# A grouped softmax on one core: four tiles instead of six, loops that cover all rows, and no inner block barrier

## Chip, cores and metric

One core of one Trainium2 chip. The metric is the device time in microseconds (us).

## The reference

The input is 4 x 4096 x 4352 float32. Each row of 4352 is split into 8 groups of 544, and a softmax is taken over each group.

```python
x_g = x.reshape(B, N, 8, 544)
x_g = x_g - x_g.max(axis=-1, keepdims=True)
exp = np.exp(x_g)
out = exp / exp.sum(axis=-1, keepdims=True)
```

Every element is read once and written once. The arithmetic is a maximum, an exponential with a sum, and a scaling.

## The kernel before

The 16384 rows are cut into 64 tiles. A tile has 128 partitions with two rows of 4352 each (4352 KB). "Row" below means one row on all 128 partitions, so there are 128 rows of work. The sync engine's queue issues all loads and stores. The vector engine takes the maximum and scales, and the scalar engine exponentiates. All arithmetic is in place in the tile.

```python
R = 2; NT = 6; S = R * NT
turns = (nr - 1) // S                    # nr = 128 rows: 10 turns of 12 rows, 8 rows left
...
ctx.enter_context(nc.cleanup_on_exit())  # clears the semaphores, then a barrier
...
with nc.Block(no_gpsimd_drain=True) as block:
    def load(t):                         # sync engine
        b = t % NT
        if t >= NT:
            sync.wait_ge(stored[b], 16 * (t // NT))
        sync.dma_start(out=bufs[b][:, :], in_=xt[t]).then_inc(landed[b], 16)
    for t in range(NT - 1):
        load(t)
    for t in range(nt):                  # nt = 64 tiles
        sync.wait_ge(scaled, R * (t + 1))
        sync.dma_start(out=ot[t], in_=bufs[t % NT][:, :]).then_inc(stored[t % NT], 16)
        if t + NT - 1 < nt:
            load(t + NT - 1)
    ...
    vector_max(0)                        # vector engine
    with loop(vector):                   # the loop's head is placed (head_slot)
        for s in range(S):
            vector_max((s + 1) % S)      # runs one row ahead, also across the loop's end
            vector_scale(s)
    for n in range(turns * S, nr): ...   # the unrolled rest; the scalar engine alike
```

`vector_scale(s)` waits for the exponentials of row s, takes 8 reciprocals in one instruction, and multiplies each group. In program order the queue issues store t, then load t + NT - 1. That load waits until store t - 1 has landed, because it goes into the same buffer.

## Time and profile before

| | before |
|---|---|
| time, median of the first 3 runs | 1330.53 us (1330.25 to 1331.39) |
| span of the profiled run | 1328.7 us |
| bytes moved | 570.43 MB in 128 transfers |
| DMA engines busy | 99.6% |
| vector / scalar engine busy | 78% / 58% |

The prediction shows the lines of the profile that carry this table. They are read in this order: which resource is always busy (the DMA engines), what the queue that feeds them waits for, and then the order of events at the start, in the middle and at the end.

### The profile page before, as it was taken

What the parts mean: (1) busy time and instruction counts of PE and PEld (TensorE: products, weight loads), DVE (VectorE), ACT (ScalarE), POOL (GpSimd) and SP (SyncE); (2) the same over time, 40 slices, a digit from 0 to 9 for tenths busy, and PEclk for the clock granted to TensorE, in tenths of its full rate; (3) what the DMA queues carried; (4) which work ended last, traced back from release to release, by engine and by line L of the source; (5) the groups of instructions that cost most, each with busy time, mean ns of one, the idle gap of its engine ahead of it and who ended that gap; (6) DMA issues with size and microseconds to landing.
All of it is one profiled execution on the core that took longest, in us unless ns stands there. A gap on an engine that the chain in (4) does not pass through costs nothing. (4 is left out here: it accounts for less than half of the span.)

```text
span 1328.7 us, 4036 instructions
## 1 busy us (share of the span) xinstructions
DVE 1041.5 (78%) x1280; ACT 764.4 (58%) x2049; POOL 0.2 (0%) x4
## 2 busy tenths in 40 slices
DVE  5999987787877878778778787787877877878770
ACT  3777765655656556555565565655655556556560
POOL 0000000000000000000000000000000000000000
DMA  9999999999999999999999999999999999999997
GB/s 401 418 434 434 434 430 428 432 436 433 435 433 431 429 436 434 436 435 430 429 436 434 435 435 432 428 435 435 434 436 434 429 431 436 434 435 434 431 430 336
DMA packets 18441, 570.51 MB, mean 429 GB/s; under 512 B 2048, under 2 KB 2048, under 8 KB 2048
## 3 DMA queue, kind: packets, MB, share of 16 engines
q1 hardware_dynamic: 18432, 570.43, 99.6%
q14 instruction: 9, 0.07, 0.0%
HBM read 285.21 MB, written 285.21 MB: 429 GB/s over the span
## 5 line engine op out<-in xcount | busy, mean ns | idle before, releaser
L72 ACT ACTIVATE xt<-xt,mx 128x544 f32<-128x544 f32 x1024 | 751.3, 735 | 528.7 <-ACTq L69 528.7
L56 DVE TENSOR_REDUCE mx<-xt 128x8 f32<-128x4352 f32 x128 | 599.1, 4680 | 234.0 <-DVEq L55 233.1
L64 DVE TENSOR_SCALAR xt<-xt,rs 128x544 f32<-128x544 f32 x1024 | 434.0, 497 | 19.2 <-DVEq L61 0.9
L72 ACT ACTIVATION_READ_ACCUMULATOR xt<-xt,mx 128x1 f32 x1024 | 191.1, 187 | 0.0
L60 DVE RECIPROCAL rs<-sm 128x8 f32<-128x8 f32 x128 | 24.5, 191 | 3.2 <-DVEq L59 3.2
L123 ACT ACT_TABLE_LOAD x1 | 1.3, 1283 | 0.9 <-SPq L36 0.9
L143 POOL MEMSET const-bfloat16-1.0<- 128x1 bf16 x1 | 0.1, 102 | 0.0
L143 POOL MEMSET const-uint8-127<- 128x1 uint8 x1 | 0.1, 102 | 0.0
L143 POOL MEMSET const-float32-0.0<- 128x1 f32 x1 | 0.1, 99 | 0.2 <-issue 0.2
L143 POOL MEMSET const-float32-1.0<- 128x1 f32 x1 | 0.1, 99 | 0.0
## 6 DMA issues: line engine op xcount, KB each, us to landing
xt<-in_x_dram SPq DMA_DIRECT2D x64, 4352.0 KB, 30.8
out_dram<-xt SPq DMA_DIRECT2D x64, 4352.0 KB, 40.7
```

The source lines that it names most:

```text
L56: nc.vector.reduce_max(out=mx[:, s, :], in_=row(s), axis=X, negate=True).then_inc(max_done, 1)
L60: nc.vector.reciprocal(out=rs[:, s, :], in_=sm[:, s, :]).then_inc(rec_done, 1)
L64: i = nc.vector.tensor_scalar_mul(out=xr[:, g, :], in0=xr[:, g, :], scalar1=rs[:, s, g:g + 1])
L72: i = nc.scalar.activation(out=xr[:, g, :], in_=xr[:, g, :], func=Exp, bias=mx[:, s, g:g + 1], scale=1.0, accum_out=sm[:, s, g:g + 1],)
L123: scalar.preload_act_table(Exp)
L143: nc = _bacc.Bacc("TRN2", target_bir_lowering=False, num_devices=1)
```

## The change

The change makes the program simpler: loops without an unrolled rest, a smaller SBUF footprint, one barrier fewer, and semaphores cleared once.

```diff
-    NT = 6
+    NT = 4
-    turns = (nr - 1) // S
+    turns = nt // NT                     # 16 turns of 8 rows, nothing left over
-    ctx.enter_context(nc.cleanup_on_exit())
-    landed = [nc.alloc_semaphore(...) ...]
+    landed = [tc.alloc_semaphore(...) ...]   # likewise the others; cleared by the context
-    with nc.Block(no_gpsimd_drain=True) as block:   # queue, vector and scalar parts inside
+    # the same queue program, issued directly
     ...
-            vector_max(0)
-            with loop(vector):
-                for s in range(S):
-                    vector_max((s + 1) % S)
-                    vector_scale(s)
-            for n in range(turns * S, nr): ...
+    with nc.vector.Fori(0, turns):           # the head's place left free
+        for s in range(S + 1):
+            if s < S:
+                vector_max(s)
+            if s:
+                vector_scale(s - 1)          # nothing runs ahead across the loop's end
```

More of the change, by code (lines that the diff above doesn't have):

```diff
@@ L6 @@
 from concourse._compat import with_exitstack
-from concourse.ordered_engine_set import OrderedEngineSet
 @with_exitstack
@@ L27 @@
     nt = N // (P * R)
-    nr = nt * R
-    turns = (nr - 1) // S
+    turns = nt // NT
+    assert turns * NT == nt
     f32 = mybir.dt.float32
@@ L34 @@
     ot = of.rearrange("(t p r) d -> t p (r d)", p=P, r=R)
+    landed = [tc.alloc_semaphore(f"landed{b}") for b in range(NT)]
+    stored = [tc.alloc_semaphore(f"stored{b}") for b in range(NT)]
+    max_done = tc.alloc_semaphore("max_done")
+    exp_done = tc.alloc_semaphore("exp_done")
+    rec_done = tc.alloc_semaphore("rec_done")
+    scaled = tc.alloc_semaphore("scaled")
     ctx.enter_context(tc.tile_critical(no_gpsimd_drain=True))
-    ctx.enter_context(nc.cleanup_on_exit())
     bufs = [ctx.enter_context(nc.sbuf_tensor(f"xt{b}", [P, R * D], f32)) for b in range(NT)]
@@ L41 @@
     rs = ctx.enter_context(nc.sbuf_tensor("rs", [P, S, G], f32))
-    landed = [nc.alloc_semaphore(f"landed{b}") for b in range(NT)]
-    stored = [nc.alloc_semaphore(f"stored{b}") for b in range(NT)]
-    max_done = nc.alloc_semaphore("max_done")
-    exp_done = nc.alloc_semaphore("exp_done")
-    rec_done = nc.alloc_semaphore("rec_done")
-    scaled = nc.alloc_semaphore("scaled")
     def row(s):
@@ L80, in scalar_exp @@
         i.then_inc(exp_done, 1)
-    def loop(engine):
-        return nc.Fori(
-            0, turns, engines=OrderedEngineSet([engine.engine]), head_slot={engine.engine: 0})
-    with nc.Block(no_gpsimd_drain=True) as block:
-        @block.sync
-        def _(sync):
-            def load(t):
-                b = t % NT
-                if t >= NT:
-                    sync.wait_ge(stored[b], 16 * (t // NT))
-                sync.dma_start(out=bufs[b][:, :], in_=xt[t]).then_inc(landed[b], 16)
-            for t in range(NT - 1):
-                load(t)
-            for t in range(nt):
-                sync.wait_ge(scaled, R * (t + 1))
-                sync.dma_start(out=ot[t], in_=bufs[t % NT][:, :]).then_inc(stored[t % NT], 16)
-                if t + NT - 1 < nt:
-                    load(t + NT - 1)
-            for b in range(NT):
-                sync.wait_ge(stored[b], 16 * ((nt - b + NT - 1) // NT))
-        @block.vector
-        def _(vector):
-            vector_max(0)
-            with loop(vector):
-                for s in range(S):
-                    vector_max((s + 1) % S)
-                    vector_scale(s)
-            for n in range(turns * S, nr):
-                if n + 1 < nr:
-                    vector_max((n + 1) % S)
-                vector_scale(n % S)
-        @block.scalar
-        def _(scalar):
-            scalar.preload_act_table(Exp)
-            with loop(scalar):
-                for s in range(S):
-                    scalar_exp(s)
-            for n in range(turns * S, nr):
-                scalar_exp(n % S)
@@ new lines, in load, with store @@
+    def load(t):
+        b = t % NT
+        if t >= NT:
+            nc.sync.wait_ge(stored[b], 16 * (t // NT))
+        nc.sync.dma_start(out=bufs[b][:, :], in_=xt[t]).then_inc(landed[b], 16)
+    def store(t):
+        nc.sync.wait_ge(scaled, R * (t + 1))
+        nc.sync.dma_start(out=ot[t], in_=bufs[t % NT][:, :]).then_inc(stored[t % NT], 16)
+    for t in range(NT - 1):
+        load(t)
+    for t in range(nt):
+        store(t)
+        if t + NT - 1 < nt:
+            load(t + NT - 1)
@@ L132 @@
+    for b in range(NT):
+        nc.sync.wait_ge(stored[b], 16 * turns)
+    nc.scalar.preload_act_table(Exp)
+    with nc.scalar.Fori(0, turns):
+        for s in range(S):
+            scalar_exp(s)
+    with nc.vector.Fori(0, turns):
[4 more added lines that the diff above has]
+                vector_scale(s - 1)
 _INS = ['x']
```

## The prediction

> **What bounds the kernel now.** I read the page first, then what the DMA queue waits for, then the vector engine and the queue in order of time. The busy rows decide little: the vector engine is busy 78%, the scalar engine 58%, and the DMA engines nearly always.
>
> ```profile
> span 1328.7 us, 4036 instructions
> ...
> DVE 1041.5 (78%) x1280; ACT 764.4 (58%) x2049; POOL 0.2 (0%) x4
> ...
> DMA  9999999999999999999999999999999999999997
> ...
> q1 hardware_dynamic: 18432, 570.43, 99.6%
> ...
> xt<-in_x_dram SPq DMA_DIRECT2D x64, 4352.0 KB, 30.8
> out_dram<-xt SPq DMA_DIRECT2D x64, 4352.0 KB, 40.7
> ```
>
> The DMA digit is 9 in every slice but the last, and the packets fill 99.6% of the 16 engines' span. So the bound is 128 transfers of 4352 KB each. What the queue waits for says the same: it waits for stores to land, hardly ever for arithmetic.
>
> ```profile
> SPq L96 <- DMA out_dram<-xt: 1141.2, 58, 20.7
> SPq L102 <- DVE xt L64: 102.4, 6, 33.3
> ```
>
> 58 of 59 later loads wait for a store to free their buffer. A store waits for arithmetic only six times, at the start and at the end. In order of time the queue and the vector engine read:
>
> ```profile
> 0.95 3.24 SPq L96 DMA_DIRECT2D xt<-in_x_dram  x5
> 37.53 0.35 SPq L102 DMA_DIRECT2D out_dram<-xt  x1
> 37.92 0.43 SPq L96 DMA_DIRECT2D xt<-in_x_dram  x1
> ...
> 596.25 4.69 DVE L56 TENSOR_REDUCE mx<-xt 128x8 f32<-128x4352 f32 x1 [3.98 <-DVEq L55]
> ...
> 616.82 4.68 DVE L56 TENSOR_REDUCE mx<-xt 128x8 f32<-128x4352 f32 x1 [3.99 <-DVEq L55]
> 621.43 0.19 DVE L60 RECIPROCAL rs<-sm 128x8 f32<-128x8 f32 x1
> 621.77 3.39 DVE L64 TENSOR_SCALAR xt<-xt,rs 128x544 f32<-128x544 f32 x8
> ...
> 1274.97 4.68 DVE L56 TENSOR_REDUCE mx<-xt 128x8 f32<-128x4352 f32 x1 [3.99 <-DVEq L55]
> ...
> 1294.49 3.39 DVE L64 TENSOR_SCALAR xt<-xt,rs 128x544 f32<-128x544 f32 x8
> ```
>
> To see: five loads go out at once, and the first store only at 37.53 us, when tile 0 is scaled. In the steady stretch one tile passes each 616.82 - 596.25 = 20.57 us, 10.28 us per transfer, and the vector engine idles 3.98 us of it. The last tile lands at about 1274.9 and is scaled by 1294.49 + 3.39 = 1297.9 us.
>
> **What the Trainium skill says.** "DMA: Bandwidth & Descriptors", Specifications, gives a fabric ceiling of 435 GB/s for the 16 engines. The trace agrees: 2 x 4352 KB (8.91 MB) in 20.57 us is 433 GB/s, so the steady stretch cannot get faster. The same page, Queues, rings and completion order, says that each engine consumes its descriptors in ring order. The trace agrees: a load lands 30.8 us after issue, which is 3 x 10.28, and a store 40.7, about 4 x 10.28, as in a first-in first-out line with two or three transfers ahead. "Runtime: NRT & Kernel Launch", Instruction fetch mechanics, warns that a taken branch out of the two-page window forces a fetch. The page here counts 9 instruction packets in all, though both loops turn 10 times, so no refetch per turn is seen before; the changed loops can test it.
>
> **The change, part by part.** Bytes, transfers, arithmetic and the alternation of loads and stores stay. I follow four parts.
>
> 1. *Four tiles, steady stretch.* Store t must be in the line before the DMA engines have emptied it. With four tiles the line after load t is store t-2, load t+1, store t-1, load t+2, store t: four transfers, 41.1 us, lie between the end of load t and the start of store t. The arithmetic of a tile, from its landing to its last scaling, takes 625.16 - 596.25 = 28.9 us, since the second row's scaling comes after the next tile's maximum. A landing comes up to some 4.2 us after most of the engines have finished that load (trace records: one engine lags), and a first packet about 1.0 us after the issue. Margin: 41.1 - 4.2 - 28.9 - 1.0 = 7.0 us. The load's side has more: load t+3 is released when store t-1 lands and still has two transfers (20.6 us) ahead. So four tiles still keep the line full. Six tiles held more than was needed: 30.8 + 28.9 + 40.7 = 100.4 us fits in five periods (102.8), and the sixth tile lay ready behind the queue's wait. Cost: 0.
>
> 2. *The loop's seam, every 8 rows.* The maximum of a turn's first row no longer runs ahead of the last scalings. For the last tile of a turn, from its landing: maximum 4.7, the previous tile's scaling to 8.3, maximum to 13.0, scaling to 16.5, then the wait for the exponentials (8 x 0.73 us after 13.1, to 19.2), scaling to 22.9 us. It is ready 6 us earlier than the others. The next tile, landed at 20.57, starts at about 23.1, 2.5 us late; its first row is scaled by 37.8 us, still before the landing after it at 41.1. So the delay is gone within that tile. 16 seams cost 0, and even a fetch of 3 us per turn would be hidden.
>
> 3. *The start.* Only three loads go out ahead of the first store. By the packet records the fourth transfer begins at 33.5 us, which is where most engines will have emptied the line. The first store goes out at 37.5 us as before (maximum, exponential and scaling of rows 0 and 1 are the same chain and need only tiles 0 and 1), first packet at 38.5. Idle: 38.5 - 33.5 = 5.0 us. After that it stays full: store 1 is ready at 54.0 and needed at 59, store 2 at 70.5 against 79.8, store 3 at 85 against 100. Cost: +5.0 us. Before, load 4 and load 5 filled this hole.
>
> 4. *The end.* Before, stores 59 to 63 lay behind the last load, and the line stayed full to the end: last landing 51.4 us after the last load's landing T (1274.83 to 1326.24 in the landing records). Now only stores 61, 62 and 63 lie behind it. Store 62 is ready at T + 8.3, in time for the lagging engine (free at T + 9.9). Store 63 is issued at T + 23.1 into an empty line (store 62 ends by T + 20.2); a lone transfer takes 13.5 us from issue to landing, as the first load did (0.95 to 14.45). So the end is T + 36.6, where a full line would give -0.4 + 3 x 10.28 + 0.3 = T + 30.8. Cost: +5.8 us.
>
> 5. *Barriers and clearing.* After the last landing the old program needs 1328.7 - 1326.2 = 2.5 us for three barriers and the clearing of semaphores. One or two barriers of some 0.4 us go, and one at the start perhaps. Gain: -0.7 us, an estimate.
>
> Check: T moves by two transfers (two of the five stores now come before the last load) and the hole: 1274.8 + 20.6 + 5.0 = 1300.4; + 36.6 = 1337.0; + 2.5 - 0.7 = 1338.8 span. The timed median lies 1.8 us over the span (1330.53 against 1328.7): **1340.5 us**, a ratio of 1.0075.
>
> **The rivals.** (a) *Four tiles are too few; the steady stretch leaves the DMA bound.* For it: the margin of 7 us is a third of a period, and five of six tiles were in use. Against: the cycle of one buffer is 30.8 + 28.9 + 13.5 (a lone store) = 73.2 us, under 4 x 20.57 = 82.3. Were I wrong by a few us of latency beyond the margin, each would cost up to 64 times: 1 us per tile is +64 us, 5% slower.
> (b) *The seam costs each turn*, by refetching the loop, whose head is no longer aligned, or by a drain. For it: the loops on both engines now have free placement. Against: the 2.5 and 3.3 us of slack computed above, and the store's own margin. If it were exposed, 16 x 2 us = +32 us, 2.4%.
> (c) *No change or faster.* If the engines started tile 0 sooner, or if the hole at the start merely let the lagging engine catch up (it is 1 us behind at 34.6), and the barriers weighed more, the sum could fall to +5 us, 1335. Faster by 2% would need a DMA rate above 433 GB/s, against the ceiling; nothing in the change offers that.
>
> **Range and chances.** Start hole 5.0 ± 1.2, end hole 5.8 ± 1.5, barriers -0.7 ± 0.5, lag of the slowest engine ± 1.5: about ± 3 us around 1340.5. I widen upward for (a) and (b): 1335 to 1347. Slower than 1357 (2%) only through (a) or (b): 0.06. Faster than 1304: 0.01. Within 2%: 0.93.
>
> **What would show it.** Right: the DMA row full except in the second and the last two slices; three loads at once at the start, then store 0 at about 37.5 us; intervals of 20.57 us between loads in the middle, released by stores, not by scaling; store waits for arithmetic in the start and for the last two or three stores only; last store alone, landing some 13.5 us after issue; every fourth tile's first maximum waiting for nothing. Wrong: the queue waiting for scaling (its store line) all along the run, or intervals over 20.6 us in the middle, which is (a); idle of the vector or scalar engine put down to issue at each seam together with such intervals, which is (b); DMA share of 99% with three loads at the start, which would say that the holes were not there.

## The result, and the profile after

The changed kernel takes 1338.24 us (median of 6 runs, 1337.47 to 1340.25), and the kernel before takes 1330.55 beside it. The ratio is 1.0059 (95% interval 1.0046 to 1.0072): 0.6% slower, clear of noise and inside the 2%. A ratio is the mean time of one kernel's fast runs over that of the other's of the same rounds, so it is not quite the ratio of the medians quoted. The profiled run was the slowest of the six, 1340.25 us with a span of 1338.5.

The page of the changed kernel has these lines. The DMA row shows 40 slices of 33.5 us each, in tenths of busy time:

```profile
span 1338.5 us, 4025 instructions
...
DMA  9899999999999999999999999999999999999996
...
q1 hardware_dynamic: 18432, 570.43, 99.0%
q14 instruction: 3, 0.02, 0.0%
```

The bytes are the same. The only slices under 9 are the second and the last; all between are as full as before. (A full row alone does not settle that nothing was lost there, see `two_ahead`; the pace of the transfers, below, does.) There are three instruction packets, fewer than the nine before, so no refetching of the loops is seen.

What the queue waits for (engine and line, what ended the wait, us in total, times, longest):

```profile
SPq L90 <- DVE xt L63: 1101.0, 64, 34.7
SPq L86 <- DMA out_dram<-xt: 178.3, 59, 8.0
```

The kernel before had 1141.2 us of waits for stores to land. Now the queue waits for scaling 64 times, 1101 us in all, and yet the middle slices of the DMA row are full. A wait of the queue is not idle time of the DMA engines: while the queue waits, they still have transfers in the line.

The queue's issues in order of time, at the start and at the end:

```profile
0.95 1.33 SPq L86 DMA_DIRECT2D xt<-in_x_dram  x3
36.95 0.35 SPq L90 DMA_DIRECT2D out_dram<-xt  x1
37.34 0.43 SPq L86 DMA_DIRECT2D xt<-in_x_dram  x1
...
1290.26 35.55 SPq L90 DMA_DIRECT2D out_dram<-xt  x3
```

Three loads go out, and nothing more until 36.95 us. At the end there are three stores, the last at 1325.47 (issues x3 spread over 35.55 us). The DMA engines in stretches of 2 us (stretch and length, busy time and instructions of three engines, clock, DMA share, GB/s):

```profile
34.00:36.00 2.00, 2.00 (x6) 2.00 (x7) 0.00 (x0) 1.00 0.00 0
...
1322.00:1324.00 2.00, 1.94 (x5) 0.00 (x0) 0.00 (x0) 1.00 0.00 0
1324.00:1326.00 2.00, 1.45 (x4) 0.00 (x0) 0.00 (x0) 1.00 0.00 0
```

These are the two holes: no packet starts, because the next transfer is a store whose tile is still being computed. The hole at the end has a second part: from 1306 to 1311.7 us, ahead of store 62, only 2 to 5 of the 16 engines had a packet, the slow ones, which were behind. What this part costs was not measured apart. From the packet and landing records, for the two profiled runs:

| | before | after | difference |
|---|---|---|---|
| fourth transfer's first packet | 33.52 | 37.79 | +4.3 (start) |
| first packet of transfer 17 | 168.43 | 173.58 | +5.2 (start, with its aftermath) |
| first packet of transfer 125 of 128 | 1280.13 | 1285.54 | +5.4 (start and middle) |
| last landing | 1326.24 | 1337.16 | +10.9 |
| span | 1328.7 | 1338.5 | +9.8 (the exit: 2.5 to 1.3 us) |

So the start costs 4.3 us of empty line and 0.9 more in the transfers right after it, the long middle only 0.3, the end 5.5, and the exit gives back 1.2. The seam of the loops is seen in the vector engine's waits for the exponentials, first the kernel before, then the changed kernel:

```profile
DVE rs L60 <- DVEq L59: 3.2, 2, 2.6
```

```profile
DVE rs L59 <- DVEq L58: 67.6, 32, 2.6
```

Two waits at each of 16 seams sum to 67.6 us, while the kernel grew by some 8. The vector engine had that time to spare.

### The profile page after: what moved, and what is told of

Same layout as the page of the kernel before. It is cut to its first block, busy times and chain, and to the rows that moved or that the text cites. A ratio compares the mean times of both kernels' runs of the same rounds, so it can differ in the third digit from the quotient of the medians.

```text
span 1338.5 us, 4025 instructions
## 1 busy us (share of the span) xinstructions
DVE 1043.4 (78%) x1280; ACT 763.2 (57%) x2049; POOL 0.2 (0%) x4
## 5 line engine op out<-in xcount | busy, mean ns | idle before, releaser
L59 DVE RECIPROCAL rs<-sm 128x8 f32<-128x8 f32 x128 | 25.0, 195 | 67.6 <-DVEq L58 67.6
## 6 DMA issues: line engine op xcount, KB each, us to landing
out_dram<-xt SPq DMA_DIRECT2D x64, 4352.0 KB, 22.5
```

Source lines behind the costliest of these rows:

```text
L59: nc.vector.reciprocal(out=rs[:, s, :], in_=sm[:, s, :]).then_inc(rec_done, 1)
```

## The experiments

**Theory.** The loss is two holes in the line of transfers, one at each end, which follow from having three loads ahead of the first store and two other stores behind the last load. The seams, the middle and the barriers matter little. **Rivals:** the seams cost the time; or four tiles are too few in the middle. Twelve runs, all correct.

**Undoing one part at a time.** `tiles4_old` is the kernel before with `-NT = 6 +NT = 4`, so it has no seam.

> The kernel before with its tile count alone set to 4 (inner block, clearing and the maximum that runs ahead across the loop's end all stay). My theory: the loss is the three loads ahead of the first store and the nearly lone last store, both there with 4 tiles whatever the loop looks like, so it keeps the changed kernel's loss and adds the old exit: 1338.2 + about 1.1 = 1339.3 us, and the queue waits for scaling at nearly every store. Rival, the seam of the loop every 8 rows costs the time: then this kernel, which has no seam, falls back to about 1331 us.

Measured: 1340.04 us, ratio 1.0068 (1.0054 to 1.0082). The loss is there without the seam and without the new loops, so the tile count makes it. The seam is not what costs.

`tiles5_old` is the same with `+NT = 5`.

> The kernel before with 5 tiles. My theory: four loads go out at once, 4 x 10.28 + 2 = 43 us of transfers, longer than the 37.5 us to the first store, so no hole at the start; four stores lie behind the last load, so the last store is issued (23.1 us after the last landing) before the line is empty (30 us), no hole at the end: 1330.5 us, the same as with six tiles, within 0.7 us. Rival, fewer buffers cost in proportion in the steady stretch: about halfway between six and four tiles, 1335 us.

Measured: 1331.91 us, ratio 1.0005 (0.9991 to 1.0019). The loss is not proportional: within the noise it vanishes with one more tile, though the median is 1.4 us over the 1330.5 expected, for a stated 0.7.

`six_noblock` keeps six tiles and the old loops, but without `nc.Block` and `cleanup_on_exit`, with `tc.alloc_semaphore`.

> Six tiles, the old loops with their unrolled rest, but the new form without the inner block and with the semaphores cleared by the context. My theory: it saves only the exit's barrier and one clearing, 2.5 us after the last landing become 1.3: 1329.4 us. Rival, leaving out the block changes the start or the queue's pace as well: more than 2 us off 1330.5 in either direction.

Measured: 1330.89 us, ratio 0.9997 (0.9984 to 1.0011). The interval holds both no gain and the 1.1 us expected (0.9992). The trace shows the exit shortened (last landing 1327.87, span 1329.3, so 1.4 us for 2.5), but the timing cannot resolve it.

**Filling each hole.** `load3_first` issues the fourth load, whose buffer is empty at the start, before the first store:

```diff
-    for t in range(NT - 1):
+    for t in range(NT):
         load(t)
     for t in range(nt):
         store(t)
-        if t + NT - 1 < nt:
+        if NT <= t + NT - 1 < nt:
             load(t + NT - 1)
```

> The changed kernel with one thing moved: the fourth tile's load, whose buffer is empty at the start, is issued with the first three instead of after the first store. My theory: the hole at the start (about 4.5 us, from the end of the third load to the first packet of the first store) is filled: 1338.2 - 4.5 = 1333.7 us. Rival, the hole only lets the slowest DMA engine catch up and costs nothing: 1338 us, unchanged.

Measured: 1333.88 us, ratio 1.0024 (1.001 to 1.0038); 1.0059 - 1.0024 of 1330.6 us is a gain of 4.7 us. The stretch that was empty is now at work:

```profile
34.00:36.00 2.00, 2.00 (x6) 2.00 (x7) 0.00 (x0) 1.00 0.68 296
```

`split_last` sends the last store in two halves, each when its row is scaled:

```diff
+        if t == nt - 1:
+            for r in range(R):
+                nc.sync.wait_ge(scaled, R * t + r + 1)
+                nc.sync.dma_start(out=ot[t][:, r * D:(r + 1) * D],
+                                  in_=bufs[t % NT][:, r * D:(r + 1) * D]).then_inc(...)
+            return
```

> The changed kernel with the last store cut into its two rows, each sent when its row is scaled (16.6 and 23.1 us after the last landing). My theory: the first half fills the hole ahead of the second, the last landing comes about 31 us after the last load's landing instead of 34.8: 1338.2 - 3.9 = 1334.3 us. Rival, the end is bound by the slowest DMA engine's lag (5 us) and not by the last store's issue: 1338 us, unchanged.

Measured: 1334.66 us, ratio 1.003 (1.0016 to 1.0044), a gain of 3.9 us as expected.

`both` has the two edits together.

> The fourth load first and the last store cut in two, together. My theory: the two holes are separate and add: 1338.2 - 4.5 - 3.9 = 1329.8 us, just under the kernel before. Rival, they are one and the same slack of the slowest engine: the gain of the larger alone, 1333.7 us.

Measured: 1331.33 us, ratio 1.0007 (0.9993 to 1.0021), a gain of 6.9 us for an expected 8.4. Each ratio's interval is some 1.8 us to either side, so the two are not told apart. It was run again beside the changed kernel.

> The changed kernel itself once more, timed beside the repaired versions on one chip, so that the gains of filling the holes can be read without a change of session: 1338.2 us, within 1 us.

Measured: 1338.09 us (1337.88 to 1338.34), ratio 1.0054 (1.004 to 1.0068).

> The fourth load first and the last store cut in two, once more, in the session of the changed kernel, because the two gains (4.7 and 3.9 us against the kernel before) summed to 8.5 but gave 6.9 together. My theory: the holes are separate and add up, the missing 1.6 us are run to run scatter of the slowest engine's lag: 1329.8 us. Rival, part of the two holes is the same slack of the slowest engine: 1331.3 us again, while the changed kernel is at 1338.2.

Measured: 1330.41 us (1329.77 to 1331.57), ratio 0.9999 (0.9986 to 1.0013), 7.7 us under the changed kernel of the same session. The gain of the larger edit alone (4.7) is ruled out, so the holes are mostly separate. Whether the last microsecond is lost in the engines' lag or in scatter stays open. This version is level with the kernel before and needs only four tiles; none of the versions beat it.

**More seams.** `seam_each_tile` has the seam's order after every tile: two maxima, then two scalings, in the loop's body.

```diff
-        for s in range(S + 1):
-            if s < S: vector_max(s)
-            if s: vector_scale(s - 1)
+        for s in range(S):
+            vector_max(s)
+            if s % R == R - 1:
+                for r in range(s - R + 1, s + 1):
+                    vector_scale(r)
```

> The changed kernel with the seam's order after every tile (two maxima, then two scalings) and not only after every fourth: 48 seams more. My theory: a seam leaves the vector and scalar engines 20.5 us per tile against 20.57 us of transfers, so the steady stretch stays just DMA bound, the first store is ready 2.4 us earlier and the last one 2.5 us earlier: 1338.2 - 4.9 = 1333.3 us, or up to 3 us more if the arithmetic's 20.5 us turns out a little over 20.57. Rival, a seam costs time of its own (a branch or refetch is not in it, only the order): 0.3 us or more for each, 1353 us or more.

Measured: 1336.15 us, ratio 1.004 (1.0027 to 1.0054). Four times the seams made the kernel 2 us faster, not slower, at the upper edge of what was expected. Starts of the two maxima of two successive tiles:

```profile
606.22 9.27 DVE L55 TENSOR_REDUCE mx<-xt 128x8 f32<-128x4352 f32 x2
...
626.66 9.27 DVE L55 TENSOR_REDUCE mx<-xt 128x8 f32<-128x4352 f32 x2
```

A tile takes 626.66 - 606.22 = 20.44 us of arithmetic, only 0.13 under the 20.57 of its transfers. The vector engine waits for a landing only once, at the start, and never catches up what it was behind then: the arithmetic itself sets the end (13.7 us to the first landing + 64 x 20.43 = 1321.2, where the last store is issued, + 11.7 to its landing).

**How near the margin is.** `tiles3_old` is the kernel before with `+NT = 3`.

> The kernel before with 3 tiles. My theory of the margin: the line then holds only store t-1 and load t+1 between load t and store t, and store t needs the landing of load t+1 plus 8.3 us of arithmetic, so the DMA engines idle some 9.7 us in each period (8.3 + 1.0 for the issue + 0.4 for the receipt): 20.6 + 9.7 = 30.3 us per tile, about 1330 + 64 x 9.7 = 1950 us. Rival, the margin of 7 us with four tiles degrades gradually, so three tiles cost a like few us: under 1400 us.

Measured: 2022.76 us (one run). The loss is not a few us, as the rival has it; the theory's mechanism holds, but its size was off: 31.5 us per tile, not 30.3. The queue, and below it the vector engine's next landing:

```profile
605.73 0.34 SPq L102 DMA_DIRECT2D out_dram<-xt  x1
606.12 0.43 SPq L96 DMA_DIRECT2D xt<-in_x_dram  x1
637.22 0.34 SPq L102 DMA_DIRECT2D out_dram<-xt  x1
```

```profile
628.86 4.69 DVE L56 TENSOR_REDUCE mx<-xt 128x8 f32<-128x4352 f32 x1 [14.92 <-DVEq L55]
637.11 4.68 DVE L56 TENSOR_REDUCE mx<-xt 128x8 f32<-128x4352 f32 x1
```

A store issued at 605.73 and the load behind it, into an empty line, are through at 628.86: 23.1 us, where I had reckoned 20.6 + 1.4 = 22.0. Then come 8.3 us of arithmetic, and the next store goes out: a closed round of 31.5 us.

`two_ahead` is the changed kernel with the maximum two rows ahead of the scaling.

```diff
-        for s in range(S + 1):
+        for s in range(S + 2):
             if s < S: vector_max(s)
-            if s: vector_scale(s - 1)
+            if s > 1: vector_scale(s - 2)
```

> The changed kernel with the maximum running two rows ahead of the scaling instead of one, so that a tile's arithmetic takes 8.25 us longer from its landing (37.1 us for 28.9). My theory: this overdraws the margin for the DMA engines that run ahead, but the slowest engine, which sets the end and is some 5 us behind them, still never finds the line empty (41.1 - 37.1 - 1.0 = 3 us left), so the middle stays at 20.57 us per tile; only the first store (40.2 for 36.95 us) and the last tiles (end about 3.9 us later) cost: 1338.2 + 3.3 + 3.9 = 1345.4 us. Rival, the margin of 7 us stated in the prediction, counted for the engines ahead, is what matters: 1.2 to 2 us per tile, 1338 + 80 to 130 = 1420 us or more.

Measured: 1391.15 us, ratio 1.0455 (1.0439 to 1.0471). Both expectations missed: mine of 1345 by 46 us, and the rival's of 1420 as well. Two successive turns of the vector engine's loop:

```profile
601.16 9.27 DVE L55 TENSOR_REDUCE mx<-xt 128x8 f32<-128x4352 f32 x2
...
686.56 9.27 DVE L55 TENSOR_REDUCE mx<-xt 128x8 f32<-128x4352 f32 x2
```

That is (686.56 - 601.16) / 4 = 21.35 us per tile, so the middle no longer runs at the transfers' 20.57. Yet its page has these lines:

```profile
DMA  9899999999999999999999999999999999999996
...
q1 hardware_dynamic: 18432, 570.43, 98.3%
...
HBM read 285.21 MB, written 285.21 MB: 411 GB/s over the span
```

The DMA row is, digit for digit, that of the changed kernel. The loss lies mostly in slower packets, which count as busy: in the packet records from 200 to 1200 us one packet of 34816 bytes took 1333 ns in the mean, against 1289 in the changed kernel; why was not tested. What shows the loss is the pace, here 411 GB/s over the span against 426. My theory that the slowest engine still keeps the middle at 20.57 us fell. What I had not counted is that a landing is only seen when the slowest engine is done, and that this landing releases the next scaling. In the changed kernel's profiled run the 16 engines' completions of one transfer spread over 6.5 us (at 636.8 to 643.3, from the landing records; 4.5 there in its repeat, `after_again`); here they spread over some 3.0 us, never over 3.5. The new theory was a closed round, and it was put to one test with a forecast.

`tiles5_two_ahead` is `tiles5_old` with the same two rows ahead (`vector_max(1)` before the loop, `vector_max((s + 2) % S)` in it).

> Five tiles in the old form, with the maximum two rows ahead of the scaling as in the run that took 1391 us with four tiles. New theory, a closed round: from a store's issue, through the load issued behind it, to that load's landing takes 23.0 us when nothing waits in the line (three tiles show it: 31.5 us per tile less 8.4), then comes the arithmetic up to the next store of this round (8.4 us one row ahead, 16.6 us two rows ahead) and the spread of the DMA engines; with n tiles the round may take n - 2 periods of 20.57 us. Four tiles two ahead: 23.0 + 16.6 + 3 = 42.6 us against 41.1, measured 2 x 21.35. Five tiles two ahead: 39.6 + 6 = 45.6 against 61.7 us, so nothing is lost: 1331.9 us within 1.5. Rival, running two rows ahead costs by itself (for instance by keeping the vector and scalar engines apart): 1380 us or more.

Measured: 1331.79 us, ratio 1.0007 (0.999 to 1.0024). With one more tile the 4.5% are gone, so running two rows ahead does not cost by itself. This run also has the old loop, without a seam, so a cost of the seam together with two rows ahead is not excluded by it. The trace of `two_ahead` bounds that. A round, from a store's issue to that of the second store after it, must fit into 41.1 us. It takes 42.35 us where no seam lies in between and 43.15 where one does (means from 100 to 1250 us). So the round is too long without a seam as well: each turn loses 1.2 and 2.0 us, and the seam adds some 0.8 of these 3.2. One round read in full: store at 679.37, the load behind it landed at 705.66, next store of the round at 722.41. The round against what is allowed:

| tiles, rows ahead | round, us | allowed, us | time per tile |
|---|---|---|---|
| 3, one | 23.1 + 8.3 = 31.4 | 20.6 | 31.5 measured |
| 4, one | 31.4 + 6.5 spread = 37.9 (profiled run) | 41.1 | 20.6 measured |
| 4, two | 23.0 + 16.6 + 3.0 = 42.6 | 41.1 | 21.35 = 42.7 / 2 measured |
| 5, two | 39.6 + 6 = 45.6 | 61.7 | no loss measured |

The first row is where the 23 us come from, and the 3.0 us of the third row is a spread read from that run (the round itself is measured above), so only the last row was forecast. That the spread adds to the round in full is an assumption.

## Why the prediction was right

The time was predicted as 1340.5 us (1335 to 1347) and measured as 1338.24. By its own steps:

1. *Four tiles, cost 0 in the middle.* Right: most engines' packets come at the same pace, 10.29 us per transfer from the 17th to the 121st in both traces. The margin of 7.0 us was too kind, because the lag of 4.2 us in it was read too small: in the trace of the kernel before, the last landing already comes 5.4 to 5.9 us after that of most engines from 328 us on. In the changed kernel the spread at mid-run was 6.5; with that the margin is 41.1 - 6.5 - 28.9 - 1.0 = 4.7, and the round of the table leaves 41.1 - 37.9 = 3.2. The margin was sound in kind and a size in it was off; that the error was smaller than the margin was in part luck. `two_ahead` shows that the rival "four tiles are too few" was near.
2. *The seam, cost 0.* Right, shown by `tiles4_old` (same loss without it) and `seam_each_tile` (four times as many, and faster). The first tile of a turn started 2.4 us late (landed at 581.5, begun at 583.93), predicted 2.5. (In rival (b) this 2.5 is called slack; it is the delay, and only the 3.3 are slack.)
3. *The start, +5.0.* Right in mechanism: 4.3 us of empty line in the trace, 5.2 with the transfers right after it, and 4.7 regained by `load3_first`. The first store went out at 36.95 us and not 37.5, since the first tile was at work 0.6 us earlier; why it landed earlier I did not test.
4. *The end, +5.8.* Right: 5.5 as the difference of the profiled runs. The last store left 1325.47 - 1302.40 = 23.1 us after the last landing, as stated. The lone transfer took 11.7 us and not 13.5: that term was 1.8 us too large. In the profiled run, the slowest of the six, the last load landed 2.0 us later than reckoned (1302.40 for T = 1300.4), so the two cancelled. In the repeat `after_again`, which took 1338.11 us, it landed at 1300.26 as reckoned, and the last store 34.75 us later instead of 36.6. So this term and the exit are nearly all of the 2.3 us by which the forecast was over the median. Filling this hole by halves regained 3.9.
5. *Exit, -0.7.* -1.2 in the trace; below what timing resolves.

Two signs that I gave for being wrong were themselves wrong. "DMA share of 99% with three loads at the start" is what the page shows (99.0%), and the holes were there all the same: some 10 us are only 0.8% of the span, so this share could not tell. And "the queue waiting for scaling (its store line) all along the run" happened, 64 times and 1101 us, and cost nothing in the middle. The queue runs in program order and names only the wait that ended last. Before, a store took 40.7 us to land and the queue met that wait first. With four tiles a store lands in 22.5 us at the median, and scaling comes last instead. Only the pace of the loads, or the bytes moved per us, tells whether the bound has moved; the DMA row did not tell it in `two_ahead`. Of the signs for being right, the dip in the last two slices came only in the last.

## What to carry to other kernels

In a kernel bound by its transfers, as this one is, buffers beyond those that keep the line full buy nothing in the middle; what fewer buffers cost shows first at the two ends, where issuing every load that has an empty buffer and splitting the last store win most of it back. Before taking a buffer away, add up the closed round (store issued, load behind it landed, arithmetic up to the store that this landing releases, spread of the DMA engines) and compare it with the periods that the buffers allow: here it was 38 us against 41, and three tiles were 52% slower. A long wait in an issuing queue is no evidence of a bound while the transfers keep their pace. Read that pace in bytes per us or in us per transfer, not in the engines' busy share: with two rows ahead the share was still 98.3% in a kernel 4.5% slower.

## What the Trainium skill lacked or had wrong

- The Trainium skill's page "DMA: Bandwidth & Descriptors", section "Why a DMA increments its semaphore by 16 and not by 1", says that the engines finish independently, but gives no size. Here the 16 completions of one transfer lay within 0.7 us at the start. In the middle they lay 6.5 us apart in the changed kernel's profiled run, with three engines late, and 4.5 us apart in its repeat, with seven late. Which engines lag, and why, was not tested.
- The same page, "Anatomy of one DMA", states a fixed cost of about 2.0 us for a DMA issued on the gpsimd path, and has no such whole figure for the sync engine's queue used here. Here a lone 4352 KB store took 11.7 us from issue to landing, against 10.28 in a full line, so 1.4 us more; a store and a load into an empty line took 23.1 against 20.6.
- The same page, "Where 436 GB/s comes from", says that for transfers between HBM and SBUF the HBM side binds at about 358 GB/s. As it stands this does not hold for one core running alone: the trace shows 433 GB/s over nearly the whole span. The page's own single-core table, just above that sentence, also goes beyond 358, so it is the sentence that lacks the condition.
- No page tells how to size the number of buffers from a closed round; the runs give 2022.8 us for three tiles, 1340.0 for four and 1331.9 for five.
